# One decoder layer with retention in chunks of 128, transposes by halves, and gates and biases of the down product in front of the first expert

## The chip, the cores and the metric

The kernel runs on one core of a Trainium2 chip. The metric is device time in microseconds (us), the median over the runs of one execution each: 1484.77 us for the kernel before, in three runs between 1484.51 and 1488.26.

## The reference, cut to what matters

One layer over 512 tokens of width 1024, in float32. Eight heads of 64 do stick-breaking attention and eight do retention; their outputs share one output projection. Then a mixture of 32 experts, four per token, and a gate on a second input of 256 per token.

```python
xn = rmsnorm(x); proj = xn @ w_in                    # 1024 -> 7 * 512
sb_q, sb_k, sb_v, r_q, r_k, r_v, r_g = split(proj)   # 512 columns each, 8 heads of 64
y_a = stick_breaking(rmsnorm(sb_q), rmsnorm(sb_k), sb_v)
y_b = retention(rope(rmsnorm(r_q)), rope(rmsnorm(r_k)) / 8, r_v)
y_b = group_norm(y_b) * silu(r_g)                    # mean and variance over a head's 64
x = x + concat(y_a, y_b) @ w_out
hn = rmsnorm(x)
x = x + moe(hn)                                      # top 4 of 32, clamped SwiGLU, 1024 wide
x = x + (p @ w_ple_proj) * sigmoid(rmsnorm(x) @ w_ple_gate)

def retention(q, k, v):                              # per head, chunks of c = 128, g = 1 - 2**(-5-h)
    inner = (q k^T * dmat) v                         # dmat[i, j] = g**(i-j) for i >= j, else 0
    kv    = (k * g**(c-1-j))^T v                     # 64 x 64 per chunk
    state = g**c * state + kv                        # scan over the chunks
    cross = (q state_before) * g**(i+1)
    return inner + cross

def moe(xt):
    gates = softmax(top_k(xt @ w_router + b_router, 4))
    for each expert e, for its tokens xb:
        glu, lin = split(xb @ w_up_gate[e] + b_up_gate[e])   # 1024 -> 2 * 1024
        h = min(glu, 7) * sigmoid(1.702 * min(glu, 7)) * (clip(lin, -7, 7) + 1)
        y[tokens] += gate * (h @ w_down[e] + b_down[e])      # 1024 -> 1024
```

## The kernel before

**In front of the experts.** The tokens are four tiles of 128 (NT = 4), the heads are paired (NP = 4 pairs of 64 + 64 partitions). A projection is done in three products of rounded halves (`mm3`, L163 to L165: high by high, low by high, high by low), and the halves of the weights are split on ScalarE and VectorE (L158, L159). In this part the scheduler of the tile framework sets the order on each engine from dependences and priorities, so the order of the program text is not the order of the engines. The pieces around the change are, in the order in which TensorE comes to them:

- `ret_qk` (L326) projects the retention queries and keys, takes each head's norm (`headnorm_rstd`, tile rrk), rotates them on VectorE (tiles nrk, mrk) and transposes them to rqT and rkT (`to_T`). For the queries the norm's factor is multiplied on here (L343); for the keys it is kept as the column rkr.
- `val` projects the values (tiles pjvR from the split weights wsvR0 to wsvR7); L580 to L582 subtract each head's mean over its 64 values, which is the mean that the group norm would take off.
- The retention loop (L593 to L632) runs over the pairs. For every chunk b of 128 keys it makes a score product rz of these keys with all queries from b on, so 512, 384, 256 and 128 columns (L607); VectorE multiplies it by the key's factor and by dec (L613), which ScalarE makes as an exponential of dif, the distance with a large value where the key is later; and a product ry with the values adds to the pair's output over the same columns (L618). The pair's two heads stand on different halves of the array's rows or columns. Then come the square (rsq), its mean per head as a product with a constant (var, L625), two table functions, gain, bias and the gate gD, and the split into yB.
- `wo_half` (L635) is the output projection. Its first half (on yA, from the attention, tiles pjo, 96 matmuls) needs nothing of the retention, and the scheduler fills it in between; the second half needs yB. The halves of its weights are woh and wol.

**The experts.** From L857 on the four compute engines run in the order in which the program is written (`manual_schedule`). Expert e has its tokens gathered to C = 96 rows (`dispatch`: a product rk spreads the ranks, VectorE makes the indices, GpSimd gathers xg from hn_d). Its 12 MiB of weights come in six pieces of 2 MiB into a ring of nine slots; pieces 0 to 3 are the up product's and 4 and 5 the down product's. `load_behind(e, c)` issues, on SyncE's queue, the load of the piece that takes over the slot of piece c, so a load begins once the products that read this slot are done.

- `turn` (L914) transposes xg in two halves of four 128-column blocks (px), each copied to xT by ScalarE; `turn_in` (L1081) does it for the next expert while the current one is at work.
- `up` (L1092) is glu and lin of the first 64 tokens, and `up32` (u) that of the other 32, where an expert has over 64 tokens. `act_in` and `act_out` make h on VectorE and ScalarE.
- `h_T` (L1149) transposes a half of h (two blocks, ph) and VectorE copies it to hT; `down` (L1157) multiplies by w_down (yb), `down32` the other 32 (yc).
- The transposes take their PSUM bank from `dbank` (L887), which hands out banks 2 and 3 in turn.
- `gates_T` (L841) transposes the gates of a tile of 128 tokens (pg, into gt), and `down_bias` (L849) adds the experts' down biases to the sum acc as a product of gt with the 32 biases bd (pb). Tiles 0 and 1 are done ahead of the loop; tiles 2 and 3 at its beginning: the transposes behind the row transposes of expert 0, the products inside its up product (L1301, L1304). `rows_of_y` makes, on VectorE, the row numbers by which each token later collects its experts' outputs.

The order in an expert is: up, act, up32, loads behind pieces 0 to 3, both halves of the next expert's row transposes, first half of h, two down products of four pairs, second half of h, the next two, act32, dispatch of the expert after next, the last four, rows out, down32, loads behind pieces 4 and 5.

## Time and profile before

| | before |
|---|---|
| median of three runs | 1484.77 us |
| profiled execution, device time | 1485.39 us |
| its span | 1483.5 us |
| PE busy | 91% |
| DVE (VectorE) busy | 30% |
| ACT (ScalarE) busy | 20% |
| POOL (GpSimd) busy | 12% |
| DMA, mean over the span | 320 GB/s |
| granted TensorE clock, mean | 0.985 |

All trace numbers are of this one profiled execution, 1485.39 us by the clock of the runs and 1483.5 us from its first to its last instruction. PE is a matmul on TensorE. A float32 matmul leaves two records in the trace (one per pass), one in the rounded format leaves one. The granted clock is a share of full speed: 1.00 is 2.4 GHz and 0.50 is 1.2 GHz. In a timeline a row is a start, a length, the engine, the line, the operation with the tiles out<-in, their shapes, how many records the row gathers, and in brackets how long the engine had stood idle before it and what ended that. Ends of matmuls are modelled, and the next one begins before the end of the last; so a run of matmuls is measured from start to start.

### The profile page before, as it was taken

Reading aid. Unit: us, or ns where it says so; the run is one execution under the profiler, and the core shown is the slowest. Engines: PE = TensorE matmul, PEld = TensorE weight load, DVE = VectorE, ACT = ScalarE, POOL = GpSimd, SP = SyncE. Lnnn points to the kernel's source line nnn. Section 1 sums busy time; section 2 is a strip of 40 time slices with the busy share of each in tenths; the row PEclk is TensorE's granted clock in tenths of the full one; section 3 lists DMA queues with packets and bytes.
Section 4 is the critical chain, followed back from the end, with each engine's and each line's share of the span. In section 5 each row is a group of like instructions: output and inputs, shape, how many; then the busy total and the mean of one; then the engine's idle time right before and its main releaser. Section 6 shows DMA issues by size and latency. Waiting matters only on the chain. (4 is left out here: it accounts for less than half of the span.)

```text
span 1483.5 us, 21634 instructions
## 1 busy us (share of the span) xinstructions
PE 1353.6 (91%) x8629; PEld 652.0 (44%) x8629; DVE 451.4 (30%) x1033; ACT 293.3 (20%) x564; POOL 182.4 (12%) x268
## 2 busy tenths in 40 slices
PE   8999999997999999999988899878999889799788
PEld 6776775463333334334333333323333333233256
DVE  4657497545111111111211111111111121032353
ACT  5645674341010000000000001000000000111133
POOL 3132000011110111010101011000111100212230
PEclk9999999998999999999999999999999999999999
DMA  7202504167999999999999999999999999989931
GB/s 286 85 29 79 143 25 170 38 250 278 362 375 410 408 390 403 413 411 414 412 392 411 410 408 412 411 397 417 408 410 394 374 413 408 398 346 403 420 131 57
DMA packets 65528, 474.81 MB, mean 320 GB/s; under 512 B 9485, under 2 KB 10033, under 8 KB 32401
## 3 DMA queue, kind: packets, MB, share of 16 engines
q1 hardware_dynamic: 54192, 441.69, 74.7%
q0 software_dynamic: 11200, 31.22, 6.0%
q8 instruction: 97, 1.59, 0.4%
q14 instruction: 39, 0.31, 0.1%
HBM read 454.40 MB, written 18.48 MB: 319 GB/s over the span
## 5 line engine op out<-in xcount | busy, mean ns | idle before, releaser
L1161 PE MATMUL yb<-ring,hT 128*64 128x512 f32 x1024 | 245.6, 612 | 35.3 <-DVE hT L1154 27.4
L1103 PE MATMUL glu<-ring,xT 128*64 128x512 f32 x1024 | 247.6, 599 | 16.3 <-DMA ring<-in_w_up_gate_dram 16.3
L1103 PE MATMUL lin<-ring,xT 128*64 128x512 f32 x1024 | 245.5, 594 | 0.0
L1139 DVE TENSOR_SCALAR gl<-glu 128x512 f32<-128x512 f32 x32 | 22.1, 692 | 530.7 <-PE glu L1103 530.7
L1103 PEld LDWEIGHTS glu<-ring,xT 128*64 128x64 f32 x1024 | 81.9, 138 | 145.5 <-issue 115.8
L1103 PEld LDWEIGHTS lin<-ring,xT 128*64 128x64 f32 x1024 | 83.0, 137 | 139.5 <-issue 139.5
L1161 PEld LDWEIGHTS yb<-ring,hT 128*64 128x64 f32 x1024 | 65.7, 137 | 152.8 <-issue 100.8
L903 POOL DMA_INDIRECT xg<-hn_d,idx x32 | 30.5, 954 | 781.3 <-DVE idx L902 469.0
L1117 PE MATMUL u<-ring,xT 128*32 128x256 f32 x2048 | 113.3, 379 | 0.0
L1140 ACT ACTIVATE sg<-gl 128x512 f32<-128x512 f32 x32 | 20.1, 629 | 408.8 <-DVE gl L1139 408.8
L1117 PEld LDWEIGHTS u<-ring,xT 128*32 128x32 f32 x2048 | 61.6, 110 | 47.4
L1174 PE MATMUL yc<-ring,hv 128*32 128x256 f32 x1024 | 58.6, 381 | 8.3 <-DVE hv L1170 8.3
L1185 ACT COPY y<-yb 128x512 f32<-128x512 f32 x31 | 18.1, 585 | 231.9 <-PE yb L1161 222.1
L920 ACT COPY xT<-px 128x384 f32<-128x384 f32 x64 | 27.7, 482 | 155.5 <-PE px L919 155.4
L1174 PEld LDWEIGHTS yc<-ring,hv 128*32 128x32 f32 x1024 | 31.6, 110 | 31.3 <-DVE hv L1170 12.1
L919 PE MATMUL px<-ident,xg 96*128 96x96 f32 x256 | 28.9, 258 | 15.4 <-PEq L1314 8.1
L1187 POOL DMA_DIRECT2D y_d<-y x62 | 33.7, 548 | 68.7 <-ACTq L1334 39.1
L919 PEld LDWEIGHTS px<-ident,xg 96*128 96x128 f32 x256 | 23.2, 145 | 34.9 <-issue 24.2
L1181 POOL DMA_DIRECT2D y_d<-yv x64 | 31.6, 501 | 54.5 <-ACT yv L1179 48.4
L1403 PE MATMUL o<-gh,z 128*128 128x512 f32 x128 | 37.3, 400 | 0.2 <-ACT z L1360 0.2
L899 DVE SCALAR_TENSOR_TENSOR scr<-rk,slot,iot 96x512 bf16<-96x512 f32 x32 | 23.9, 746 | 40.9 <-PE rk L893 40.9
L1141 DVE TENSOR_TENSOR gl<-gl,sg 128x512 f32<-128x512 f32 x32 | 22.2, 692 | 24.4 <-ACT sg L1140 23.7
(960 smaller groups left out, 1694.5 us busy)
## 6 DMA issues: line engine op xcount, KB each, us to landing
ring<-in_w_up_gate_dram SPq DMA_DIRECT2D x127, 2048.0 KB, 23.6
ring<-in_w_down_dram SPq DMA_DIRECT2D x128, 1024.0 KB, 23.0
ring<-in_w_in_dram SPq DMA_DIRECT2D x12, 1024.0 KB, 5.3
y_d<-y POOLq DMA_DIRECT2D x62, 128.0 KB, 9.7
ring<-in_w_out_dram SPq DMA_DIRECT2D x4, 1024.0 KB, 6.7
ring<-in_w_ple_gate_dram SPq DMA_DIRECT2D x2, 2048.0 KB, 22.0
y_d<-none SPq DMA_DIRECT2D x2, 1984.0 KB, 12.0
ring<-in_x_dram SPq DMA_DIRECT2D x4, 512.0 KB, 5.4
```

The lines of the kernel that those rows point to most:

```text
L899: nc.vector.scalar_tensor_tensor(scr[0:n], rk[0:n], slots[0:n], iot[0:n], op0=ALU.is_equal, op1=ALU.mult, accum_out=idf[0:n])
L903: nc.gpsimd.indirect_dma_start(out=xg[0:n], out_offset=None, in_=hn_d, in_offset=bass.IndirectOffsetOnAxis(ap=idx[0:n, :1], axis=0))
L919: nc.tensor.transpose(pv[:, k, :], xg[0:n, (4 * h + k) * P:(4 * h + k + 1) * P], ident[0:n, 0:n])
L920: nc.scalar.copy(xT[:, 4 * h:4 * h + 4, 0:n], pv)
L1103: nc.tensor.matmul(o[two(j)], xTs[e][:, 2 * m + c, 0:64], w[:, c, f:f + 512], start=False, stop=m == 3 and c == 1)
L1117: nc.tensor.matmul(u32[four(q), g * 256:(g + 1) * 256], xTs[e][:, 2 * m + c, 64:C], w[:, c, f:f + 256], start=False, stop=m == 3 and c == ...
L1141: nc.vector.tensor_tensor(gl, gl, sg, op=ALU.mult)
L1161: nc.tensor.matmul(y64[two(j)], hT[:, fc, :], w[:, fc % 4, j * 512:(j + 1) * 512], start=fc == 0, stop=fc == KD - 1)
L1174: nc.tensor.matmul(y32[four(q), 0:256], hT[:, fc % 2, fc // 2, :], w[:, fc % 4, q * 256:(q + 1) * 256], start=fc == 0, stop=fc == KD - 1, ...
L1181: nc.gpsimd.dma_start(y_d[e * C + 64:(e + 1) * C, q * 256:(q + 1) * 256], y[four(q)])
L1187: nc.gpsimd.dma_start(y_d[e * C:e * C + 64, j * 512:(j + 1) * 512], y[two(j)])
L1403: nc.tensor.matmul(banks[t, h], (zh, zl, zh)[i][:, k, ts], (g_h, g_h, g_l)[i][k // 4][:, k % 4, hs], start=first, stop=last)
```

## The change

**Retention.** The keys get their factor on VectorE before the transposes, and both queries and keys an exponential of the place in the chunk besides (`decay`: g to the plus place for queries, g to the minus place for keys), multiplied into the eight small columns of the norm (L332). So neither the column rkr nor the exponentials dec are needed. A score product is one chunk of 128 by itself (L629), four per head in one bank, and VectorE multiplies a head's four by one mask of zeros and ones (`causal`). The rest goes over states: for chunks 0 to 2, eight products of 64 by 64 (kv, L609) from the unturned keys and the values, with the sum and the factor `tile_decay` on VectorE (st); a cross product per head and chunk from 1 on (L638) and an inner product per head and chunk (L644) write the pair's output, 128 columns each. Square, var and what follows stay.

**Gates and biases.** `gates_T` and `down_bias` of tiles 2 and 3 stand ahead of the row transposes of expert 0, and the two calls inside its up product are gone.

**Transposes in halves.** `turn_in` takes a half h; the order is now first half of the next rows, first half of h, second half of the rows, second half of h, and then all eight pairs of the down product in one piece. `dbank` turns over three banks, 2 to 4.

```diff
     def ret_qk(w, name, key, tag, ahead=0):
         ns = evacuate(proj(w, name, ahead), name)
         dst = early.tile([P, NP, S], F32, name=name + "T", tag=tag)
-        rst = early.tile([P, NT, NH], F32, name=name + "r")
         for t in range(NT):
             n = ns[t]
-            r, _ = headnorm_rstd(n, f"{name}{t}", rst[:, t, :])
+            r, _ = headnorm_rstd(n, f"{name}{t}")
+            nc.vector.tensor_tensor(r, r, decay[key], op=ALU.mult)
...
             nc.vector.tensor_tensor(n, n, m, op=ALU.add)
-            if key == "q":
-                nc.vector.tensor_tensor(nv, nv, r[:, :, None].to_broadcast([P, NH, HD]), op=ALU.mult)
+            nc.vector.tensor_tensor(nv, nv, r[:, :, None].to_broadcast([P, NH, HD]), op=ALU.mult)
             to_T(n, dst, t, None, f"{name}{t}")
-        return dst, rst
+        return dst, ns
...
-    dif = early.tile([P, S], F32, name="dif")
-    nc.gpsimd.iota(dif, pattern=[[1, S]], base=0, channel_multiplier=-1, allow_small_or_imprecise_dtypes=True)
-    msk = e2.tile([P, S], F32, name="msk", tag="tmp")
-    nc.vector.tensor_scalar(msk, dif, 0.0, 1.0e6, op0=ALU.is_lt, op1=ALU.mult)
-    nc.vector.tensor_tensor(dif, dif, msk, op=ALU.add)
+    lng = [math.log(1.0 - 2.0 ** (-5.0 - h)) for h in range(NH)]
+    place_col = early.tile([P, 1], F32, name="place_col")
+    nc.gpsimd.iota(place_col, pattern=[[0, 1]], base=0, channel_multiplier=1, allow_small_or_imprecise_dtypes=True)
+    decay = {}
+    for key, sign in (("q", 1.0), ("k", -1.0)):
+        decay[key] = early.tile([P, NH], F32, name="decay" + key)
+        for h in range(NH):
+            nc.gpsimd.memset(decay[key][:, h:h + 1], sign * lng[h])
+        nc.scalar.activation(decay[key], decay[key], AF.Exp, scale=place_col)
+    tile_decay = early.tile([P, NP], F32, name="tile_decay")
+    for h in range(NH):
+        nc.gpsimd.memset(tile_decay[h % 2 * HD:h % 2 * HD + HD, h // 2:h // 2 + 1], math.exp(P * lng[h]))
+    causal = early.tile([P, P], F32, name="causal")
+    nc.vector.tensor_scalar(causal, jp, 0.0, None, op0=ALU.is_ge)
...
-    rkT, rkr = ret_qk(w_rk, "rk", "k", "kT", 200)
+    rkT, rkn = ret_qk(w_rk, "rk", "k", "kT", 200)
...
+    hss = [slice(j * HD, (j + 1) * HD) for j in range(2)]
+    kvb = [bank(6 + i, f"kv{i}") for i in range(2)]
+    states = []
+    for b in range(NT - 1):
+        kv = kvb[b // 2][:, b % 2 * 256:b % 2 * 256 + 256]
+        for h in range(NH):
+            nc.tensor.matmul(kv[hss[h % 2], h // 2 * HD:h // 2 * HD + HD], rkn[b][:, h * HD:(h + 1) * HD],
+                             vR[:, b, h * HD:(h + 1) * HD], start=True, stop=True)
+        st = e2.tile([P, 256], F32, name=f"st{b}", tag=("wt1", "wt1", "wt2")[b])
+        sv = st.rearrange("p (c d) -> p c d", d=HD)
+        fall = tile_decay[:, :, None].to_broadcast([P, NP, HD])
+        if b == 0:
+            nc.vector.tensor_tensor(sv, kv.rearrange("p (c d) -> p c d", d=HD), fall, op=ALU.mult)
+        else:
+            nc.vector.tensor_tensor(st, states[-1], kv, op=ALU.add)
+            nc.vector.tensor_tensor(sv, sv, fall, op=ALU.mult)
+        states.append(st)
     for hp in range(NP):
-        hss = [slice(j * HD, (j + 1) * HD) for j in range(2)]
-        decs = []
+        py = bank(4 + hp % 2, f"ry{hp}")
+        zs, scs = [], []
         for j in range(2):
-            h = 2 * hp + j
-            dec = e2.tile([P, S], F32, name=f"dec{h}", tag="tmp")
-            nc.scalar.activation(dec, dif, AF.Exp, scale=math.log(1.0 - 2.0 ** (-5.0 - h)))
-            decs.append(dec)
-        py = bank(4 + hp % 2, f"ry{hp}")
+            zs.append(zbank(f"rz{hp}{j}", (0, 1, 2, 3)))
         for b in range(NT):
-            N = S - b * P
-            zs, scs = [], []
+            ts = slice(b * P, (b + 1) * P)
             for j in range(2):
-                z = zbank(f"rz{hp}{j}{b}", (0, 1, 2, 3))
-                nc.tensor.matmul(z[:, :N], rkT[hss[j], hp, b * P:(b + 1) * P], rqT[hss[j], hp, b * P:S],
-                                 start=True, stop=True)
-                zs.append(z)
+                nc.tensor.matmul(zs[j][:, ts], rkT[hss[j], hp, ts], rqT[hss[j], hp, ts], start=True, stop=True)
+        for j in range(2):
+            sc = e2.tile([P, S], F32, name=f"rs{2 * hp + j}", tag="wt0")
+            nc.vector.tensor_tensor(sc.rearrange("p (b t) -> p b t", t=P), zs[j].rearrange("p (b t) -> p b t", t=P),
+                                    causal[:, None, :].to_broadcast([P, NT, P]), op=ALU.mult)
+            scs.append(sc)
+        for b in range(1, NT):
+            ts = slice(b * P, (b + 1) * P)
+            for j in range(2):
+                nc.tensor.matmul(py[hss[j], ts], states[b - 1][hss[j], hp * HD:(hp + 1) * HD], rqT[hss[j], hp, ts],
+                                 start=b == 1, stop=False)
+        for b in range(NT):
+            ts = slice(b * P, (b + 1) * P)
             for j in range(2):
                 h = 2 * hp + j
-                sc = e2.tile([P, N], F32, name=f"rs{h}{b}", tag=f"wt{b}")
-                nc.vector.scalar_tensor_tensor(sc, zs[j][:, :N], rkr[:, b, h:h + 1], decs[j][:, :N],
-                                               op0=ALU.mult, op1=ALU.mult)
-                scs.append(sc)
-            for j in range(2):
-                h = 2 * hp + j
-                nc.tensor.matmul(py[hss[j], b * P:S], vR[:, b, h * HD:(h + 1) * HD], scs[j],
-                                 start=b == 0, stop=b == NT - 1)
+                nc.tensor.matmul(py[hss[j], ts], vR[:, b, h * HD:(h + 1) * HD], scs[j][:, ts], start=False,
+                                 stop=b == NT - 1)
...
     def down_bias(t):
         for h in range(2):
-            pb = bank(h + (6 if t > 1 else 4), f"pb{t}{h}")
+            pb = bank(h + (6 if t == 2 else 4), f"pb{t}{h}")
...
     def dbank(name):
         dn[0] += 1
-        return bank(2 + dn[0] % 2, name)
+        return bank(2 + dn[0] % 3, name)
...
-    def turn(xg, n, xT, name):
-        for h in range(2):
+    def turn(xg, n, xT, name, halves=range(2)):
+        for h in halves:
             pt = dbank(f"px{name}{h}")
...
-    def turn_in(e):
-        xTs[e] = ringC.tile([P, KD, C], F32, name=f"xT{e}", tag="xT")
-        turn(xgs[e], C, xTs[e], f"{e}")
+    def turn_in(e, h):
+        if e < E:
+            if h == 0:
+                xTs[e] = ringC.tile([P, KD, C], F32, name=f"xT{e}", tag="xT")
+            turn(xgs[e], C, xTs[e], f"{e}", (h,))
...
+    for t in (2, 3):
+        gates_T(t)
+    for t in (2, 3):
+        down_bias(t)
     turn(xgs[0], C, xTs.setdefault(0, ringC.tile([P, KD, C], F32, name="xT0", tag="xT")), "0")
-    gates_T(2)
-    gates_T(3)
     for t in range(NT):
         rows_of_y(t)
...
         up(e, 0)
-        if e == 0:
-            down_bias(2)
         up(e, 1)
-        if e == 0:
-            down_bias(3)
...
         for c in range(4):
             load_behind(e, c)
-        if e + 1 < E:
-            turn_in(e + 1)
+        turn_in(e + 1, 0)
         h_T(h, hT, 0, f"{e}a")
-        down(e, hT, (0, 1))
+        turn_in(e + 1, 1)
         h_T(h, hT, 1, f"{e}b")
-        down(e, hT, (2, 3))
+        down(e, hT, (0, 1, 2, 3))
```

VectorE around the last splits of the value weights (wsvR5l to wsvR7l), before; nrk and mrk are tiles of the rotated keys, vm the means of the values:

```order
L159 SCALAR_TENSOR_TENSOR wsvR5l<-ring_62,pmix,wsvR5h 128x512
L341 TENSOR_TENSOR nrk_1996<-nrk_1996,mrk_2039 128x512
L338 TENSOR_TENSOR mrk_2055<-nrk_1998,stk 128x8x32
L340 TENSOR_TENSOR nrk_1998<-nrk_1998,ctk 128x512
L341 TENSOR_TENSOR nrk_1998<-nrk_1998,mrk_2055 128x512
L159 SCALAR_TENSOR_TENSOR wsvR6l<-ring_62,pmix,wsvR6h 128x512
L159 SCALAR_TENSOR_TENSOR wsvR7l<-ring_62,pmix,wsvR7h 128x512
L580 TENSOR_REDUCE vm_2216<-vR 128x8
L580 TENSOR_REDUCE vm_2220<-vR 128x8
```

The same place after (rrk is the norm's factor of a key tile, wol a split of the second output weight):

```order
L159 SCALAR_TENSOR_TENSOR wsvR5l<-ring_62,pmix,wsvR5h 128x512
L341 TENSOR_TENSOR nrk_2031<-nrk_2031,mrk_2081 128x512
L332 TENSOR_TENSOR rrk_2095<-rrk_2095,decayk 128x8
L338 TENSOR_TENSOR mrk_2100<-nrk_2033,stk 128x8x32
L342 TENSOR_TENSOR nrk_2031<-nrk_2031,rrk_2076 128x512
L340 TENSOR_TENSOR nrk_2033<-nrk_2033,ctk 128x512
L159 SCALAR_TENSOR_TENSOR wsvR6l<-ring_62,pmix,wsvR6h 128x512
L341 TENSOR_TENSOR nrk_2033<-nrk_2033,mrk_2100 128x512
L581 TENSOR_TENSOR wol_2252<-ring_63,woh_2251 128x1024
L342 TENSOR_TENSOR nrk_2033<-nrk_2033,rrk_2095 128x512
L159 SCALAR_TENSOR_TENSOR wsvR7l<-ring_62,pmix,wsvR7h 128x512
L589 TENSOR_REDUCE vm_2262<-vR 128x8
```

A factor of eight columns and a multiply over 512 columns of each key tile, and a split of wol, now stand between the splits.

TensorE behind the last value product, before:

```order
L165 MATMUL pjvR_2071<-wsvR7h,xl 128x512
L607 MATMUL rz_2259<-rqT,rkT 128x512
L607 MATMUL rz_2261<-rqT,rkT 128x512
L607 MATMUL rz_2269<-rqT,rkT 128x384
L607 MATMUL rz_2271<-rqT,rkT 128x384
L163 MATMUL pjo_2482<-woh_2205,yA 128x512
L164 MATMUL pjo_2482<-wol_2206,yA 128x512
L618 MATMUL ry_2258<-rs_2263,vR 64x512
L607 MATMUL rz_2279<-rqT,rkT 128x256
L165 MATMUL pjo_2482<-woh_2205,yA 128x512
L618 MATMUL ry_2258<-rs_2265,vR 64x512
```

The same place after (kv are the products of keys and values, st the states):

```order
L165 MATMUL pjvR_2117<-wsvR7h,xl 128x512
L629 MATMUL rz_2335<-rqT,rkT 128x128
L629 MATMUL rz_2336<-rqT,rkT 128x128
L629 MATMUL rz_2335<-rqT,rkT 128x128
L629 MATMUL rz_2336<-rqT,rkT 128x128
L609 MATMUL kv_2300<-vR,nrk_2027 64x64 x8
L629 MATMUL rz_2335<-rqT,rkT 128x128
...
L629 MATMUL rz_2376<-rqT,rkT 128x128 x4
L609 MATMUL kv_2300<-vR,nrk_2029 64x64 x8
L609 MATMUL kv_2301<-vR,nrk_2031 64x64 x8
L638 MATMUL ry_2334<-rqT,st_2310 64x128 x2
L629 MATMUL rz_2377<-rqT,rkT 128x128 x4
```

Products of 128 to 512 columns with pjo between them have become runs of 128 columns, with states and cross products in front of the first pjo.

TensorE in expert 0, its start and the turn from up to down product, before (px are transposed rows, pg gates, pb biases, ph transposes of h):

```order
L919 MATMUL px_3095<-ident,xg_3041 128x96 x4
L919 MATMUL px_3101<-ident,xg_3041 128x96 x4
L845 MATMUL pg_3108<-ident,gates 96x128
L845 MATMUL pg_3113<-ident,gates 96x128
...
L852 MATMUL pb_3209<-bd_2632,gt_3107 128x512
L852 MATMUL pb_3212<-bd_2632,gt_3107 128x512
...
L919 MATMUL px_3329<-ident,xg_3054 128x96 x4
L919 MATMUL px_3335<-ident,xg_3054 128x96 x4
L1153 MATMUL ph0a<-ident,h_3194 128x128 x2
L1161 MATMUL yb_3191<-ring_2602,hT_3195 64x512 x4
L1153 MATMUL ph0b<-ident,h_3194 128x128 x2
L1161 MATMUL yb_3191<-ring_2602,hT_3195 64x512 x4
```

and after:

```order
L871 MATMUL pg_3111<-ident,gates 96x128
L871 MATMUL pg_3116<-ident,gates 96x128
L878 MATMUL pb_3120<-bd_2648,gt_3110 128x512
L878 MATMUL pb_3123<-bd_2648,gt_3110 128x512
...
L945 MATMUL px_3133<-ident,xg_3057 128x96 x4
L945 MATMUL px_3139<-ident,xg_3057 128x96 x4
...
L945 MATMUL px_3345<-ident,xg_3070 128x96 x4
L1181 MATMUL ph0a<-ident,h_3222 128x128 x2
L945 MATMUL px_3355<-ident,xg_3070 128x96 x4
L1181 MATMUL ph0b<-ident,h_3222 128x128 x2
L1189 MATMUL yb_3219<-ring_2618,hT_3223 64x512 x8
```

Gates and biases have moved ahead of the rows; each pair of transposes of h has a half of the next rows ahead of it, and the down product is no longer cut by one.

## Rows read from the trace of the kernel before

**Rows 1.** The page's forty slices, DMA line: busy share in tenths.

```profile
DMA  7202504167999999999999999999999999989931
```

**Rows 2.** Windows, PE: stretch, length, busy (x instructions), granted clock, DMA share, GB/s.

```profile
236.08:299.18 63.10, 61.36 (x233) 1.00 0.39 137
...
340.90:349.40 8.50, 2.60 (x18) 0.50 0.65 208
```

**Rows 3.** Groups, PE, 236.08 to 299.18: busy, mean ns, idle before, releaser.

```profile
L618 PE MATMUL ry<-rs,vR 128*64 128x512 f32 (+3 forms) x64 | 18.1, 458 | 1.4 <-DVE rs L613 1.4
L607 PE MATMUL rz<-rqT,rkT 64*128 64x256 f32 (+3 forms) x64 | 17.0, 473 | 0.0
...
L625 PE MATMUL var<-rsq,gmean 128*128 128x512 f32 x8 | 4.4, 634 | 0.3 <-ACT rsq L623 0.3
```

**Rows 4.** Timeline, PE: start, length, engine, line, operation, tiles.

```profile
84.33 1.05 PE L442 MATMUL prs<-ident,rs 128*128 128x128 f32 x8
...
283.07 0.43 PE L618 MATMUL ry<-rs,vR 128*64 128x128 f32 x2
283.43 0.50 PE L165 MATMUL pjo<-woh,yA 128*128 128x512 f32 x1
...
291.02 0.40 PE L164 MATMUL pjo<-wol,yA 128*128 128x512 f32 x1
...
298.95 0.40 PE L165 MATMUL pjo<-woh,yA 128*128 128x512 f32 x1
```

**Rows 5.** Windows and timeline, DVE, projection of retention keys and values.

```profile
208.30:228.80 20.50, 19.81 (x32) 1.00 0.01 1
...
198.75 0.69 DVE L343 TENSOR_TENSOR nrq<-nrq,rqr 128x512 f32<-128x512 f32 x1
...
231.35 0.75 DVE L159 SCALAR_TENSOR_TENSOR wsvR7l<-ring,pmix,wsvR7h 128x512 fp32r<-128x512 f32 x1 [2.54 <-ACT wsvR7h L158]
```

**Rows 6.** Windows, PE, of the holes in the stream.

```profile
365.00:372.00 7.00, 7.00 (x100) 1.00 0.26 66
404.00:409.00 5.00, 5.00 (x88) 1.00 0.38 88
441.00:444.00 3.00, 1.84 (x16) 1.00 0.65 158
...
1127.00:1131.00 4.00, 4.00 (x74) 1.00 0.73 279
1164.00:1168.00 4.00, 1.65 (x11) 0.85 0.66 233
1297.00:1305.00 8.00, 6.83 (x38) 1.00 0.41 123
```

**Rows 7.** Timeline, PE, start of expert 0.

```profile
347.10 1.51 PE L919 MATMUL px<-ident,xg 96*128 96x96 f32 x8 [5.90 <-DMA xg<-hn_d,idx]
...
354.17 0.73 PE L852 MATMUL pb<-bd,gt 96*128 96x512 f32 x2
...
359.32 1.09 PE L852 MATMUL pb<-bd,gt 96*128 96x512 f32 x2 [0.83 <-DVE acc L854]
```

**Rows 8.** Timeline, PE, turn from up to down in expert 1.

```profile
412.95 0.44 PE L1153 MATMUL ph1a<-ident,h 128*128 128x128 f32 x2 [0.29 <-ACT xT L920]
413.91 1.94 PE L1161 MATMUL yb<-ring,hT 128*64 128x512 f32 x8 [0.52 <-DVE hT L1154]
...
416.73 1.94 PE L1161 MATMUL yb<-ring,hT 128*64 128x512 f32 x8 [0.52 <-DVE hT L1154]
```

**Rows 9.** Timelines, PE and DVE, expert 28.

```profile
1302.12 0.85 PE L919 MATMUL px<-ident,xg 96*128 96x96 f32 x8 [0.31 <-PEq L1314]
...
1302.65 0.42 DVE L1147 SCALAR_TENSOR_TENSOR h<-h,gl 128x256 f32<-128x256 f32 x1
```

**Rows 10.** Waits, PE, 370 to 1425: total, count, longest; timeline, expert 31.

```profile
PE glu L1103 <- DMA ring<-in_w_up_gate_dram: 16.3, 10, 2.6
...
1386.82 1.94 PE L1103 MATMUL glu<-ring,xT 128*64 128x512 f32 x8 [2.57 <-DMA ring<-in_w_up_gate_dram]
```

## The prediction, made before the changed kernel was run

> **What bounds the kernel now.** I began with the DMA line of the forty slices [rows 1]: the 16 DMA engines are nearly idle in slices 6 to 8 and full from the tenth slice to the last but two. That long stretch is the expert loop, which streams 12 MiB of weights per expert. A kernel that is full on DMA for two thirds of its time can shorten in three ways only: the stream begins earlier, it has fewer holes, or the part behind it shrinks. So I read three places. First the stretch in front of the loop, where TensorE (PE) is the bound: from 236.08 to 299.18 PE is busy for 61.36 of 63.10 us while DMA is at 0.39 [rows 2]. Then the start of the loop, where PE stands idle for the first gather (2.60 us busy of 8.50, at half the clock [rows 2]). Then the holes in the stream, cut out by windows [rows 6]; every one ends when a ring slot is released, and slots 0 to 3 of an expert are released by its up product, so by PE. The loop's end is tied to the stream: expert 31 waits 2.57 us for its weights [rows 10], and over the whole loop PE waits 16.3 us for weights, in ten waits, all of them after 760 us (the view gives the same row when it begins there) [rows 10]. So before 760 us PE sets when slots come free, and what it gains there closes holes; whatever shifts the stream shifts the end.
>
> **The retention stage.** In the 63.1 us, 96 matmuls of the first half of the output projection (pjo, the filler) step by 7.93/34 = 0.233 us [rows 4], together 22.4; waits are 1.4 + 0.3 us [rows 3]; so retention itself holds PE for 39.0 us, and the three groups rz, ry, var read 18.1 + 17.0 + 4.4 = 39.5 [rows 3]. The change replaces 64 matmuls of 128 to 512 columns by 32 score tiles, 24 state products, 24 cross and 32 inner products, 112 small ones, and keeps var. A float32 matmul leaves two records, one for each pass, so x8 in a row is four of them. Prices: four 128-column float32 matmuls in a run take 1.05 us to the last one's end, 0.25 each with the pipeline's end taken off [rows 4]; a lone one takes 0.36 until the next kind starts (283.07 to 283.43) [rows 4], so a change of kind costs about 0.11. Two matmuls on different halves of the array run together when they stand side by side (the 64 records of the score products by 473 ns would be 30.3 us and take 17.0 [rows 3]); in the order of the changed kernel 8 pairs and 16 lone score tiles, 12 pairs of cross, 16 of inner and 12 of state products do. So 24 + 12 + 16 + 12 = 64 turns by 0.25 = 16.0, var 4 by 1.1 = 4.4, and 30 changes of kind (57 before) by 0.11 = 3.3: 23.7 us, 15.3 less. The Trainium skill, page TensorEngine Tiling (Array Packing), section Key Properties, states that a change of tiling mode drains TensorE; the 0.11 agrees with that, and without it the sum would be 3.3 us lower.
>
> The bounds: with no cost for a change of kind 39.0 - 20.4 = 18.6 us are saved; with all 112 alone at 0.36, 40.3 + 4.4 = 44.7, 5.7 are lost. I take 15.3, since the order has most of them in runs. What hides the rest: the chain behind the last inner product (copy, square, var, two table functions, two vector operations, split) needs some 8 us, an estimate, and has 79 pjo by 0.233 = 18.4 us in front of it, so it stays covered. The eight exponentials and the 17 us of score scaling that go on ScalarE and VectorE lay beside PE and give nothing. One us I charge for new waits: state products wait for the centred values, cross products for the states on VectorE, which stands behind two splits of the second output weight.
>
> **The price in front of it.** The key rows now get their scale on VectorE, four more 128x512 multiplies at 0.69 [rows 5], 2.8 us, and four tiny ones. VectorE is busy for 19.81 of 20.50 us there and then has 2.54 us of air before the split of the last value weights [rows 5]. PE takes these splits as they come, and key transposes now wait for one operation more. Walking the two queues by these durations I find waits of 0.3 to 0.8 us at four places: 2 us, between 0 and 3.3. ScalarE's two small exponentials and the 24 extra fills of GpSimd at the start lie in idle time and cost nothing. The stage: 15.3 - 1 - 2 = 12 us earlier, between -9 and 19.
>
> **Gates and down biases ahead of expert 0.** Before, PE waits 5.90 us for the gather, then transposes rows, then gates, and the biases stand inside the up product: 0.73 us at 354.17, and 0.83 of waiting plus 1.09 at 359.32 [rows 7], of whose 2.65 I take 2.5, since the last pass of each runs into the next matmul. Now all this stands in the wait. The gates of the last two tiles are ready before the gather lands; at half the clock the work ends about 1 us after it, which is what the gates cost behind the transposes before. So up begins at the same time and ends 2.5 us earlier, the first slots with it; bounds 1.5 and 2.5. Nothing on VectorE is later: the bias additions move ahead of the rows of y.
>
> **Transposes in halves.** In an expert with over 64 tokens the down product waited for 0.29 (second bank of xT), 0.52 and 0.52 us (hT copies) [rows 8]; now each copy has a half of the transposes or another product over it, and three banks turn: 1.33 us less. In a light expert h comes from VectorE after the up product: its first half is ready at about 1303.05, when four transposes from 1302.12 would be done at 1302.55 [rows 9]; half a us of wait is new, so 0.86 remains. PE is not the bound everywhere, so this counts through holes alone. They lose (1 - share) times length [rows 6]: 5.2 at 365, 3.1 at 404, 1.0 at 441, 1.1 at 1127, 1.4 at 1164, 4.7 at 1297, together 16.5. The first shrinks by the 2.5 of expert 0; the next two by 1.3 and 1.0, since PE is then 1.3 us further ahead per expert; those at 1127 and 1164 stand behind three and four heavy experts in a row, 3.9 and 5.2 us of gain against 2.5, and go; of the last I take half, 2.3, as PE may run into the stream in the light experts ahead of it. 2.5 + 2.3 + 2.5 + 2.3 = 9.6, taken as 10; bounds 2.5 (expert 0 alone) and 14.
>
> **The sum.** 12 + 10 = 22 us. The profiled execution took 1485.39 us (span 1483.5), 0.6 over the median of 1484.77; 1485.4 - 22 = 1463.4, and 1463 against the median.
>
> **Rivals.** A measurement of this kernel tells about 0.3% (4.5 us) from no change.
> - Stream-bound: the holes stay, because DMA is at its limit and PE only waits in other places. For it speaks the full share between the holes; against it that each hole ends with a release by PE. Then 12 + 2.5: 1485.4 - 14.5 = 1471.
> - Better packing: changes of kind cost little in runs and the hole at 1297 closes. 19 + 14 = 33: 1452.
> - Lone matmuls: the small products don't overlap and pay 0.36 each; the stage is 5.7 + 3 = 9 slower, the loop gives 10 back: 1484, no change.
> - Slower: the cross products wait for states, these for VectorE, and PE idles between so many short products that its granted clock falls, as it does in 340.9 to 349.4 (0.50, with 2.60 us busy of 8.50 [rows 2]). The stage's 48 us at 1.2 GHz cost up to 48 more: 1463 + 48 = 1511; it decides from 22 us at the lower level. Against it: by my walk no wait in the stage is over 1 us. The Trainium skill, page TensorE: Matmul & The Clock Gate, Part 1, has the lower rate as the one an idle engine falls back to.
> - That the change does not do what it says is settled by the order: small products, halves and gates stand where the text puts them.
>
> **How the numbers follow.** Forecast 0.55 (1463, own range 1455 to 1471), stream-bound 0.18, better packing 0.16, lone matmuls 0.08, slower clock 0.03. Faster takes the first three and a corner of the fourth, 0.90; same 0.06; slower 0.04. The range reaches from the better packing to just past the stream-bound case: 1452 to 1474.
>
> **What will show it.** In the changed profile the stretch from the last value product to the last pjo of the first half should be 49 to 51 us instead of 63; the value products should be pushed back by about 2 us with waits for VectorE; glu of expert 0 should begin about 12 us earlier than 349.4 and its up product hold no bias; waits of the down product for hT should all but vanish; the DMA share at the six holes should be near 1 save the first two. I am wrong if the short products take over 0.3 us a turn, if PE's clock falls in the stage, or if the holes move instead of closing.

## The result, and the profile after

The changed kernel takes 1460.85 us (median of four runs, 1459.98 to 1462.05); the kernel before took 1486.01 beside it. The ratio is 0.983, 95% interval 0.9813 to 0.9847. The forecast was 1463. The profiled execution has a span of 1458.8 us against 1483.5, so 24.7 us are to be found.

I cut both spans at five instructions whose starts stand in the TensorE timelines: the first score product, the first product of the second half of the output projection, the first bias product of expert 0, the first product of expert 31 with its weights, and the end. The same cuts serve for every kernel below.

| us | before | after | change |
|---|---|---|---|
| up to the first score product | 236.1 | 237.1 | +1.1 |
| retention stage | 63.1 | 45.0 | -18.1 |
| from there to the loop's start | 50.2 | 50.8 | +0.6 |
| loop, to the first weights of expert 31 | 1037.4 | 1028.3 | -9.1 |
| tail | 96.7 | 97.5 | +0.8 |

The page's clock and DMA lines of after, in forty slices; the DMA line answers to [rows 1]:

```profile
PEclk9999999998999999999999999999999999899889
DMA  8201604549999999999999999999999999999921
```

The full stretch of DMA begins a slice earlier and has no dip left up to the last slice but two. The clock has new dips in three of the last six slices.

Windows on TensorE after, columns as in [rows 2]: the retention stage, and the wait in front of expert 0.

```profile
237.14:282.20 45.06, 44.39 (x330) 1.00 0.60 211
...
325.00:333.00 8.00, 4.92 (x18) 0.50 0.76 245
```

The stage holds TensorE for 44.39 of 45.06 us. Its groups (busy, mean ns, idle before them), of which the first three and the last take the place of rz and ry in [rows 3]:

```profile
L629 PE MATMUL rz<-rqT,rkT 64*128 64x128 f32 x64 | 6.9, 291 | 0.0
L644 PE MATMUL ry<-rs,vR 128*64 128x128 f32 x64 | 5.2, 280 | 0.0
L638 PE MATMUL ry<-rqT,st 64*64 64x128 f32 x48 | 4.6, 285 | 0.0
L651 PE MATMUL var<-rsq,gmean 128*128 128x512 f32 x8 | 4.3, 618 | 0.5 <-ACT rsq L649 0.5
...
L609 PE MATMUL kv<-vR,nrk 128*64 128x64 f32 x48 | 2.0, 227 | 0.2 <-DVE vR L591 0.2
```

Together 23.0 us, where [rows 3] had 39.5. The start of expert 0 after, in the timeline, which answers to [rows 7]:

```profile
328.07 1.40 PE L871 MATMUL pg<-ident,gates 128*96 128x128 f32 x4 [3.41 <-DVE gates L847]
329.48 2.30 PE L878 MATMUL pb<-bd,gt 96*128 96x512 f32 x4
331.57 1.48 PE L945 MATMUL px<-ident,xg 96*128 96x96 f32 x8
...
333.84 3.26 PE L1131 MATMUL glu<-ring,xT 128*64 128x512 f32 x8
```

The wait is now for the gates, 3.41 us; the rows follow gates and biases. The turn from up to down product in expert 1 after, against [rows 8]:

```profile
391.49 0.55 PE L945 MATMUL px<-ident,xg 96*128 96x96 f32 x4
391.87 0.39 PE L1181 MATMUL ph1a<-ident,h 128*128 128x128 f32 x2
392.09 0.49 PE L945 MATMUL px<-ident,xg 96*128 96x96 f32 x4
392.66 0.44 PE L1181 MATMUL ph1b<-ident,h 128*128 128x128 f32 x2
393.03 3.65 PE L1189 MATMUL yb<-ring,hT 128*64 128x512 f32 x16
```

The two waits of 0.52 us are gone, and of the one of 0.29 some 0.07 are left, ahead of row 392.66; the sixteen records of the down product follow each other. Over a whole expert TensorE needs 35.2 instead of 36.9 us with over 64 tokens, and 25.1 instead of 26.1 with fewer (starts of the bias products of neighbouring experts).

The windows of the holes that are left, against [rows 6]:

```profile
349.00:354.00 5.00, 5.00 (x94) 1.00 0.37 95
385.00:389.00 4.00, 4.00 (x80) 1.00 0.55 156
1262.00:1264.00 2.00, 1.97 (x13) 1.00 0.74 268
1270.00:1276.00 6.00, 5.11 (x28) 1.00 0.65 244
```

(1 - share) times length gives 3.2, 1.8, 0.5 and 2.1 us, 7.6 together, where [rows 6] gave 16.5. What TensorE waits for weights over the span, total, times and longest, against [rows 10]:

```profile
PE glu L1131 <- DMA ring<-in_w_up_gate_dram: 46.9, 24, 8.1
```

So the loop's TensorE time fell by some 42 us (16 times 1.7 and 15 times 1.0), and 30.6 us of that are new waits for weights.

### The profile page after: what moved, and what is told of

It is laid out like the page before. It is cut to its first block, busy times and chain, and to the rows that moved or that the text cites. A ratio compares the mean times of both kernels' runs of the same rounds, so it can differ in the third digit from the quotient of the medians.

```text
span 1458.8 us, 21861 instructions
## 1 busy us (share of the span) xinstructions
PE 1339.0 (92%) x8725; PEld 656.6 (45%) x8725; DVE 446.8 (31%) x1025; ACT 291.7 (20%) x558; POOL 185.7 (13%) x292
## 5 line engine op out<-in xcount | busy, mean ns | idle before, releaser
L1131 PE MATMUL glu<-ring,xT 128*64 128x512 f32 x1024 | 258.0, 624 | 46.9 <-DMA ring<-in_w_up_gate_dram 46.9
L1189 PE MATMUL yb<-ring,hT 128*64 128x512 f32 x1024 | 235.4, 602 | 0.8 <-DVE hT L1182 0.8
L929 POOL DMA_INDIRECT xg<-hn_d,idx x32 | 30.6, 957 | 765.6 <-DVE idx L928 424.1
L946 ACT COPY xT<-px 128x384 f32<-128x384 f32 x64 | 30.7, 480 | 163.4 <-PE px L945 161.9
L945 PE MATMUL px<-ident,xg 96*128 96x96 f32 x256 | 33.8, 255 | 6.5 <-PEq L1341 4.6
L945 PEld LDWEIGHTS px<-ident,xg 96*128 96x128 f32 x256 | 25.7, 143 | 26.4 <-PEq L1341 16.2
```

Of the source, the lines that this page charges most:

```text
L929: nc.gpsimd.indirect_dma_start(out=xg[0:n], out_offset=None, in_=hn_d, in_offset=bass.IndirectOffsetOnAxis(ap=idx[0:n, :1], axis=0))
L945: nc.tensor.transpose(pv[:, k, :], xg[0:n, (4 * h + k) * P:(4 * h + k + 1) * P], ident[0:n, 0:n])
L946: nc.scalar.copy(xT[:, 4 * h:4 * h + 4, 0:n], pv)
L1131: nc.tensor.matmul(o[two(j)], xTs[e][:, 2 * m + c, 0:64], w[:, c, f:f + 512], start=False, stop=m == 3 and c == 1)
L1189: nc.tensor.matmul(y64[two(j)], hT[:, fc, :], w[:, fc % 4, j * 512:(j + 1) * 512], start=fc == 0, stop=fc == KD - 1)
```

## The experiments

The first six kernels are the other combinations of the three parts, so that with before and after all eight are there. Four kernels then test single prices and waits, and two the place of the instructions.

| kernel | median us | ratio to before, interval | stage | loop | tail |
|---|---|---|---|---|---|
| before | 1484.6 to 1486.4 | | 63.1 | 1037.4 | 96.7 |
| retention alone | 1466.18 | 0.9875 (0.9847 to 0.9902) | 45.0 | 1032.8 | 98.4 |
| halves alone | 1479.75 | 0.9957 (0.9941 to 0.9972) | 63.1 | 1033.1 | 94.8 |
| gates alone | 1485.96 | 1.0004 (0.9990 to 1.0017) | 63.1 | 1038.4 | 96.2 |
| retention, halves | 1461.82 | 0.9841 (0.9819 to 0.9863) | 45.0 | 1030.0 | 98.5 |
| retention, gates | 1466.41 | 0.9867 (0.9845 to 0.9888) | 45.0 | 1032.5 | 98.4 |
| halves, gates | 1477.55 | 0.9943 (0.9921 to 0.9966) | 63.1 | 1030.7 | 94.7 |
| all three (after) | 1460.85 | 0.9830 (0.9813 to 0.9847) | 45.0 | 1028.3 | 97.5 |

**Retention alone.** The changed kernel with the old calls put back for the other two parts:

```diff
-    for t in (2, 3):
-        gates_T(t)
-    for t in (2, 3):
-        down_bias(t)
...
+    gates_T(2)
+    gates_T(3)
...
         turn_in(e + 1, 0)
+        turn_in(e + 1, 1)
         h_T(h, hT, 0, f"{e}a")
-        turn_in(e + 1, 1)
+        down(e, hT, (0, 1))
         h_T(h, hT, 1, f"{e}b")
-        down(e, hT, (0, 1, 2, 3))
+        down(e, hT, (2, 3))
```

> The kernel before with the tiled retention alone; transposes, gates and biases stand as before. Theory A (a shift in front counts in full, and the PE time saved in the loop counts only as far as it closes holes of the stream): the loop starts some 17 us earlier as in the changed kernel, its six holes stay, together about 19 us, so 1486.0 - 16.5 = 1469.5. Theory B (only the front counts; what PE saves in the loop is waited away for weights): as fast as the whole change, 1461. Theory C (packing gains little, and the loop brings most): over 1476.

1466.18, 19.0 us less than the kernel before beside it (1485.21), and 3 us less than A. The front is as A has it (loop at 333.3 against 349.4). But the loop, in which nothing was changed, is 4.6 us shorter. Windows of its last three holes:

```profile
1110.00:1114.00 4.00, 4.00 (x68) 1.00 0.79 299
1147.00:1149.00 2.00, 1.41 (x12) 1.00 0.82 262
1278.00:1283.00 5.00, 4.45 (x27) 1.00 0.69 225
```

0.8, 0.4 and 1.6 us: the earlier holes are about those of [rows 6], but these three lose 2.8 where [rows 6] had 1.1 + 1.4 + 4.7 = 7.2. B falls: 1466 is not 1461. C falls too.

**Halves alone.** The kernel before with the order and the three banks of the changed one:

```diff
-        return bank(2 + dn[0] % 2, name)
+        return bank(2 + dn[0] % 3, name)
...
-            turn_in(e + 1)
+        turn_in(e + 1, 0)
         h_T(h, hT, 0, f"{e}a")
-        down(e, hT, (0, 1))
+        turn_in(e + 1, 1)
         h_T(h, hT, 1, f"{e}b")
-        down(e, hT, (2, 3))
+        down(e, hT, (0, 1, 2, 3))
```

> The kernel before with the transposes in halves over three banks alone. A: an expert with over 64 tokens takes 35.2 us on PE instead of 36.9, one with fewer 25.1 instead of 26.1; the loop starts where it did, at 349.4; the holes at 404, 441, 1127 and 1164 close and half of that at 1297, about 7 us: 1479. B: 1486, no change, and the waits of the up product for weights grow by as much as PE saves, some 35 us. C: 1476 or less.

1479.75, as A says; the loop is 4.3 us shorter and the tail 1.9. The waits for weights do grow, from 14.3 to 44.4 us up to the first weights of expert 31, as B said as well: both hold, most of the gain is waited away and what closes holes stays. A is wrong on the last hole, though:

```profile
1288.00:1300.00 12.00, 11.06 (x53) 1.00 0.46 169
```

It loses 6.5 us, where [rows 6] had 4.7.

**Gates alone.** The kernel before with

```diff
+    for t in (2, 3):
+        gates_T(t)
+    for t in (2, 3):
+        down_bias(t)
     turn(xgs[0], C, xTs.setdefault(0, ...), "0")
-    gates_T(2)
-    gates_T(3)
...
-        if e == 0:
-            down_bias(2)
...
-        if e == 0:
-            down_bias(3)
```

> The kernel before with gates and down biases ahead of the first expert's row transposes alone. A: up of expert 0 is 2.2 us shorter and the first hole shrinks by that: 1483.8, too little to tell from no change in the time, so the trace of the first hole (365 to 372 before) decides: 3 us lost in it instead of 5.2. B: 1486, with the first hole smaller and another larger.

1485.96, no difference. The windows of its first and its last hole:

```profile
365.00:370.00 5.00, 5.00 (x96) 1.00 0.44 118
...
1294.00:1306.00 12.00, 10.84 (x50) 1.00 0.23 65
```

The first hole loses 2.8 us (5.2 before), as A has it, but the last one loses 9.2 (4.7 before). So it went as B says: the gain of 2.4 us at the beginning is taken back at the end. Experts 24 and 26 are 1.5 and 2.9 us longer there than in the kernel before; on these see below.

**Retention and halves.** The changed kernel with the last diff undone.

> The changed kernel with the gates and biases back in their old places. A: 1460.9 + 2.2 = 1463, the first hole of the stream larger by 2.2 us than in the changed kernel. B: 1461, no difference.

1461.82 against 1460.85; the intervals overlap widely. The traces differ by 1.7 us in the loop, but by the time A and B can't be told apart.

**Retention and gates.** The changed kernel with the diff of the halves undone.

> The changed kernel with the transposes in the old order over two banks. A: the holes that the halves close come back, some 7 us: 1468. B: 1461, no difference, since PE only waits less for weights.

1466.41: B falls, and A is 1.6 us high, as it was 3 us high with the retention alone, whose late holes this kernel shares.

**Halves and gates.** The kernel before with both of these diffs.

> The kernel before with gates and halves, without the tiled retention. A: the loop starts at 349.4 as before and its holes shrink from 19 to about 9 us: 1476.5. B: 1486.

1477.55, as A says, with the loop at 1030.7.

**Pairs apart.** The changed kernel with the loops over the two heads of a pair turned outside in, in all four kinds of products, as here for the scores:

```diff
-        for b in range(NT):
-            ts = slice(b * P, (b + 1) * P)
-            for j in range(2):
+        for j in range(2):
+            for b in range(NT):
+                ts = slice(b * P, (b + 1) * P)
```

> The changed kernel with each pair's first head written out ahead of its second one, so that two products on different halves of the array no longer stand side by side (scores, cross, inner and state products). If two such products run together and a pair costs one turn of 0.25 us, as the forecast has it, some 45 turns more are paid: 10 to 12 us, 1471 to 1473. If a product on half of the array costs its own time wherever it stands: 1461, and the retention stage stays at 45 us.

1461.5, ratio 0.9832 (0.9815 to 0.985), no difference in the time; the stage has 48.4 us instead of 45.0. Eight inner products (16 records) and the next row, first of this kernel, then of the changed one:

```profile
249.39 1.58 PE L644 MATMUL ry<-rs,vR 128*64 128x128 f32 x16
250.90 0.87 PE L638 MATMUL ry<-rqT,st 64*64 64x128 f32 x8
```

```profile
248.04 1.09 PE L644 MATMUL ry<-rs,vR 128*64 128x128 f32 x16
249.06 0.43 PE L638 MATMUL ry<-rqT,st 64*64 64x128 f32 x4
```

From start to start 1.51 us apart and 1.02 side by side: 0.19 us for a product alone and 0.255 for a pair. So pairs do run together, the pair's price of 0.25 was right, and the price of a product alone was not: 0.25 came from products over the whole array [rows 4], 0.19 is that of one on half of it. Some 48 fewer pairs cost 3.4 us of the stage: TensorE is busy for 48.39 us in it instead of 44.39, and 0.7 us of waits are gone. The loop starts 3.8 us later; the tail takes 1.2 of that back, and the profiled span is 2.5 us longer. The medians are only 0.65 us apart; the four runs of this kernel spread over 2.8 us, so the time alone can't show the 2.5.

**Work in the wait for the gates.** Twelve products of 512 columns from 32 rows, read by nothing:

```diff
+    warm(bank(0, "warm0"), 12)
     for t in (2, 3):
         gates_T(t)
```

> The changed kernel with 12 products of 512 columns, whose result nothing reads, on PE in the 3.4 us in which it waits for the gates of the last two tiles. If the half clock behind that idle time is what makes gates, biases and the first up products slow (0.50 from 325 to 333, 0.74 to 340), the clock stays near 1.00, the first up product is released some 2.3 us earlier and the first hole of the stream shrinks by that: 1458.6. If the hole is set by something else: 1461.

1460.07, ratio 0.9829 (0.981 to 0.9848), no difference. The timeline there:

```profile
324.86 5.48 PE L935 MATMUL warm<-rankT,ident_r 32*128 32x512 f32 x12
...
333.55 1.49 PE L949 MATMUL px<-ident,xg 96*128 96x96 f32 x8
...
335.82 2.19 PE L1135 MATMUL glu<-ring,xT 128*64 128x512 f32 x8
```

The twelve take 5.48 us, 0.46 each: the clock had fallen before they began, and it did not rise under them (0.50 from 325 to 335). They end 2.0 us too late for gates, biases and rows. In return the first up products run at full clock sooner. The test did not keep the clock up, so what that would be worth at expert 0 stays open.

**The place of the instructions.** In the kernel before and in the three others with the old retention, the row transposes in one to three light experts (64 tokens or fewer) are held up, mostly by TensorE's sequencer. A row of expert 24 before, and the sum of the sequencer's waits there over the loop (total, times, longest), before and with the retention alone:

```profile
1166.62 1.35 PE L919 MATMUL px<-ident,xg 96*128 96x96 f32 x8 [2.35 <-PEq L1314]
```

```profile
PE px L919 <- PEq L1314: 8.1, 14, 2.4
```

```profile
PE px L945 <- PEq L1343: 4.6, 15, 0.3
```

These waits lie at the branch over the 32-token part. Experts 18, 24 and 26 take 29.4, 30.5 and 28.9 us before, and 26.1 each with the retention alone. About half of that is the clock: behind each wait the next eight records of the down product take 3.60, 3.68 and 3.42 us, and not 1.94. At expert 24 (granted clock 0.50 from 1167 to 1173):

```profile
1169.16 3.68 PE L1161 MATMUL yb<-ring,hT 128*64 128x512 f32 x8 [0.52 <-DVE hT L1154]
```

The wait of expert 24 stands inside the hole at 1164, and all three ahead of the largest late one, at 1297. Two kernels test whether it is the place of TensorE's instructions that makes them. The first adds 12 products of 64 columns to the retention alone, in front of the first rows; the second 96 to the kernel before:

```diff
+    shift(bank(0, "shift"))
     turn(xgs[0], C, xTs.setdefault(0, ringC.tile([P, KD, C], F32, name="xT0", tag="xT")), "0")
```

> The tiled retention alone (1466.2) with 12 products of 64 columns, read by nothing, ahead of the first row transposes, in PE's wait for the gather. They move every later PE instruction of the program by 12 products. In the kernels with the old retention PE's sequencer holds the row transposes of experts 18, 24 and 26 up for 1.5 to 2.8 us each behind the branch over the 32-token part; with the new retention no such wait is over 0.3 us, and the loop is 4.6 us shorter although nothing in it was changed. If the place of the instructions decides this, the waits of 1.5 us or more come back here and the loop (1032.8 us from its start to the first weights of expert 31) grows to about 1037: 1470. If it is something that the retention does, nothing changes: 1466.

1467.16, ratio 0.9883 (0.9854 to 0.9913), and the loop 1032.2: the time does not change, and experts 18, 24 and 26 have no wait over 0.8 us. But the rows of experts 12 and 14 now wait 1.74 and 1.44 us, where they don't with the retention alone. The view puts these waits down to VectorE and not to the sequencer, so a sum by the sequencer's name misses them:

```profile
PE px L949 <- DVE h L1178: 1.7, 1, 1.7
```

> The kernel before with 96 such products, by which the new retention leaves more PE records than the old one (8725 against 8629), in the wait for the gather. If the place of the instructions decides: the waits of PE's sequencer at experts 18, 24 and 26 fall to 0.3 us and the loop goes from 1037.4 to about 1033, 1481.5 in all, less what the 96 products push the row transposes back (0 to 2 us). If not: 1485 to 1488, with the waits of 1.5 to 2.8 us as they were.

1500.83, ratio 1.0111 (1.0079 to 1.0142). The 96 products took far longer than I had thought, 0.216 us each:

```profile
340.34 20.69 PE L909 MATMUL shift<-rankT,ident_r 32*128 32x64 f32 x96
```

They push the loop's start back by 13.9 us; the profiled span is 12.7 us longer and the median 16.2. The loop is 1.7 us shorter (1035.7) and not the 4.4 that I had expected, since the up product of expert 0, which frees the first slots, comes later and DMA moves nothing from 361 to 372. But the waits at experts 18, 24 and 26 are gone, and with them most of the late holes, 1.2 + 0.4 + 1.6 = 3.1 us instead of 7.2:

```profile
PE px L923 <- PEq L1319: 4.3, 14, 0.3
```

```profile
1143.00:1147.00 4.00, 4.00 (x72) 1.00 0.71 270
1180.00:1182.00 2.00, 1.40 (x11) 1.00 0.81 254
1311.00:1316.00 5.00, 3.83 (x24) 1.00 0.68 219
```

The kernel with work in the wait for the gates, which is the changed one with 12 products more, waits 2.91 us at expert 12 and 2.76 at expert 18. The changed kernel itself has one such wait, of 1.58 us at expert 12, for which the trace shows no releaser ("issue"; the other of the two lies under 0.4):

```profile
PE px L945 <- issue: 1.9, 2, 1.6
```

Taken whatever the view names, these are the waits over 1 us at row transposes inside the loop, in the one execution of each kernel that was profiled. The last column is the DMA time lost from the start of expert 24 to that of expert 30: 1 less the DMA share, summed over the microseconds with a share under 0.9.

| kernels | waits: expert (us) | DMA time lost, us |
|---|---|---|
| before | 18 (1.94), 24 (2.35), 26 (1.48) | 7.0 |
| gates alone | 18 (1.97), 24 (2.19), 26 (2.02) | 11.3 |
| halves alone; halves, gates | 26 (2.76; 2.67) | 7.2; 6.9 |
| retention alone | none | 3.3 |
| retention, gates | 2 (2.17) | 3.3 |
| retention, halves; after; pairs apart; the two with work at the end (below) | 12 (1.51 to 1.87) | 2.4 to 3.1 |
| work in the wait for the gates | 12 (2.91), 18 (2.76) | 3.0 |
| retention alone, 12 products ahead | 12 (1.74), 14 (1.44) | 3.1 |
| before, 96 products ahead | 2 (2.08) | 2.7 |

So in these traces products put ahead of the loop move the waits from one expert to another. That the waits at 18, 24 and 26 can go without the new retention is shown by the 96 products. The late holes go with waits at experts 24 and 26: 6.9 to 11.3 us are lost in the four kernels that have one there, 2.4 to 3.3 in the ten that have none. Whether the waits move with the place of the instructions or with the time by which the products shift the rest is not told apart: the 12 products ahead of the retention alone bring two with the loop's start unmoved (333.2 against 333.3), which speaks against the time, but the other two kernels shift it by 13.9 and 2.0 us. With one trace of each it is not shown either that a kernel has them at the same expert in every execution; that five kernels have theirs at expert 12 speaks for it.

**Work in the waits at the end.** Products that nothing reads at three places of expert 31 where TensorE idles:

```diff
+        if e == E - 1:
+            warm(bank(5, "warm1"), 34)
         glu, lin, u32 = bank(0, f"glu{e}"), ...
...
+        if e == E - 1:
+            warm(dbank("warm2"), 14)
         with tc.If(n_e > 64):
...
         if e == E - 1:
+            warm(bank(5, "warm3"), 12)
             break
```

> The changed kernel with products that nothing reads where PE idles at the end: 34 of 512 columns ahead of expert 31, in its 8.1 us wait for weights, 14 in the wait for its activation, 12 behind its down product. If the clock falls there because PE idles (0.70 from 1361 to 1366, 0.76 from 1387 to 1396, 0.85 to 1404), it stays near 1.00 and the tail from expert 31's first weights to the end shrinks from 97.5 to about 94: 1457.5. If not, or if the products come in the way of real ones: 1461 or more.

1464.15, ratio 0.9856 (0.9828 to 0.9884), 3.3 us slower than the changed kernel. The first window, and the first up product behind it:

```profile
1353.00:1366.00 13.00, 13.00 (x38) 0.57 1.03 432
```

```profile
1364.64 3.62 PE L1135 MATMUL glu<-ring,xT 128*64 128x512 f32 x8
```

TensorE is busy without a gap and its granted clock falls all the same, to 0.57 in the mean; at half the clock the products outlast the wait by 3 us. The products used 32 of the 128 rows. So I changed that, and with it the operands (the identity on both sides) and the numbers, to 28, 10 and 10:

```diff
-            nc.tensor.matmul(pb, ident_r[0:E, 0:1].to_broadcast([E, P]), rankT, start=True, stop=True)
+            nc.tensor.matmul(pb, ident_r, ident_r[:, None, :].to_broadcast([P, 4, P]), start=True, stop=True)
```

> The changed kernel with products that nothing reads where PE idles at the end, as in the kernel before this one (1464, where the clock fell to 0.57 although PE was busy all the time with products over 32 of the 128 rows), but over all 128 rows: 28 ahead of expert 31, 10 in the wait for its activation, 10 behind its down product. If the clock goes with how much of the array is at work, it stays at 1.00 from 1352 to 1404 and the tail behind expert 31's first weights shrinks from 97.5 to about 94: 1457.5. If it falls all the same: 1462 or more, as the products then last beyond the wait.

1461.57, ratio 0.9829 (0.9811 to 0.9846). Windows, and the rows of the products, the down product and the join behind it (pc, by which expert 31's output is added to its tokens):

```profile
1353.00:1360.00 7.00, 6.26 (x30) 1.00 1.03 431
1360.00:1366.00 6.00, 3.91 (x12) 0.72 1.00 425
...
1387.00:1396.00 9.00, 8.83 (x40) 1.00 0.78 313
```

```profile
1352.11 6.59 PE L935 MATMUL warm<-ident_r 128*128 128x512 f32 x28 [0.57 <-PEq L1370]
...
1387.17 7.09 PE L1193 MATMUL yb<-ring,hT 128*64 128x512 f32 x32 [1.24 <-DVE hT L1186]
...
1399.24 0.98 PE L1232 MATMUL pc<-yl,oh 64*128 64x512 f32 x4 [2.45 <-DVEq L1466]
```

With all rows at work the clock stays at 1.00 until the products end, and falls at the end of the 2.84 us that are then left of the wait for weights (0.72). That the rows decide, and not the values in the operands, is likely but not shown. The down product runs at 1.00. The same window, and the first up product, the down product and the join, in the changed kernel:

```profile
1387.00:1396.00 9.00, 8.69 (x32) 0.76 0.76 304
```

```profile
1361.27 3.28 PE L1131 MATMUL glu<-ring,xT 128*64 128x512 f32 x8 [8.13 <-DMA ring<-in_w_up_gate_dram]
...
1387.32 9.06 PE L1189 MATMUL yb<-ring,hT 128*64 128x512 f32 x32 [0.79 <-DVE hT L1182]
1399.19 0.83 PE L1228 MATMUL pc<-yl,oh 64*128 64x512 f32 x4 [2.81 <-DVEq L1457]
```

The down product is 2.0 us shorter (7.09 against 9.06 us), and the join begins at 1399.24 against 1399.19: nothing gained. VectorE, which adds the collected rows of the other experts, ends that work there only at 1398.4, and the split of expert 31's output that the join reads (yl, 0.68 us) stands behind it in VectorE's order (its timeline in the kernel with all rows):

```profile
1393.57 4.86 DVE L1268 SCALAR_TENSOR_TENSOR acc<-gy,gk,acc 128x1024 f32<-128x1024 f32 x4
```

My 1457.5 was wrong at this step. I had taken TensorE for the last in the tail, and at the join it is VectorE.

## Why the prediction was right, point by point

**The stage.** Forecast 63.1 - 15.3 + 1 = 48.8 us, measured 45.0, below the 49 to 51 that I had named as a sign. Taking off 96 products of the filler at 0.233 (22.4) and 0.7 us of waits leaves 21.9 for the retention, where 23.7 was forecast; the rest of the 3.8 us are waits, of which I had kept the old 1.7 and added one, and found 0.7. So the mechanism was right, and two terms were a little high. The state products were the cheapest against their price: 2.0 us by their group, where 12 turns of 0.25 had been put down for them. The 0.11 us for a change of kind made 3.3 of the 23.7; without it the sum was 20.4, and 21.9 lies between. The Trainium skill, page TensorEngine Tiling (Array Packing), section Key Properties, has a change of tiling mode drain TensorE, and tiles on different parts of the array work in parallel; the pairs (0.255 against twice 0.19) agree with the second, and no run here takes the first apart from the rest.

**In front of it.** Forecast +2 us, measured +1.1; over all traces the first score product starts at 235.2 to 236.1 us with the old retention and at 237.0 to 237.9 with the new one, 1.7 us apart in the mean. The next stretch is 0.6 longer, and so the loop starts 16.4 us earlier where 12 was forecast.

**Expert 0.** Rows came about a us behind the gather, as forecast: 331.57, with the gather's landing put at 330.55 (as far behind the last product ahead of the wait as before, 6.18 us). Up then ran at half the clock longer: its first eight records need 3.26 us. From the loop's start to the end of the 64-token up product it is 16.1 us instead of 18.0, so 1.9 of the 2.5 are left. Alone the part brings nothing that shows.

**The halves.** Forecast 1.33 and 0.86 us an expert, measured 1.7 and 1.0; the down product in one piece gains besides the waits.

**The holes.** Forecast -10 for the loop, measured -9.1, and hole for hole: 3.2 at the first (forecast 5.2 - 2.5 = 2.7), 1.8 at the second (1.8), none at 441, 1127 and 1164, half of the last. The rule behind it held in all eight combinations: TensorE time in the loop is worth what it closes of holes. The loop takes 1028.3 to 1038.4 us in them; less its lost DMA time, counted as above over the whole loop, it takes 1016.7 to 1020.9. But the account by parts was wrong. I put all of the 10 down to gates and halves; alone they shorten the loop by -1.0 and 4.3 us, and the retention, which I gave none of it, by 4.6, of which 4.4 lie in the three late holes. These holes go with the waits at experts 24 and 26, in all fourteen kernels. The trace of the kernel before shows these waits (8.1 us in all, up to 2.4 at a time), one of them inside the very hole of which I wrote that a row of heavy experts was behind it. So the step that was wrong is the cause of the late holes. I had put half of the last one down to the halves; alone they leave it at 6.5 us (4.7 before), and the retention brings it to 1.6, along with the waits at experts 24 and 26, of which I had not thought. That the loop's sum came out all the same is luck.

**The tail.** I forecast no change; it is 0.8 us longer. Expert 31 waits 8.1 us for its first weights instead of 2.57 [rows 10], and its first up product and its down product then run at a reduced clock.

**The rivals.** Stream-bound (1471) falls by the halves, which bring 6.4 us alone (0.9957), and by the holes, of which 7.6 us are left of 16.5; but most of the 42 us that are saved on TensorE is indeed waited away. Lone matmuls (1484) falls by its price: apart, the products cost 3.4 us and not 21. The slower clock (1511) falls by the stage's granted clock of 1.00. Better packing (1452) was right on the stage (-18.1 of its 19) and wrong on the loop.

## What to carry to other kernels

Where a stream of weights is the bound for most of the time, look for its holes and for what each waits; time in front of the stream counts in full, compute time beside it only as far as it closes a hole. A forecast whose sum is right may still be wrong by parts: the eight combinations of three edits showed that 4.6 us of the loop come through a part that was not meant to touch it. Price a matmul on half of the array from one on half of the array.

## What was unexpected of the hardware

- The granted clock fell to 0.50 while TensorE was busy without a gap, with products of 512 columns from 32 rows (mean 0.57 over 13.00 us, all busy); with products of the same columns from all 128 rows and other operands it stayed at 1.00. The Trainium skill, page TensorE: Matmul & The Clock Gate, Part 1, has the lower rate as that of an idle engine; the fall in the 2.84 us of waiting agrees, the fall under 34 products without a gap is beyond it.
- The row transposes behind the branch over the 32-token part are held up by 1.4 to 2.9 us at up to three experts of a kernel and by 0.3 at most others, and which experts these are changes with what was put hundreds of us ahead. The loss doubles where the granted clock falls behind the wait (3.68 us for eight records instead of 1.94).
- Products of 64 columns from 32 rows take 0.216 us each in a row of 96 (20.69 us) behind idle time, at a granted clock of 0.50 from the first to the last: small products are not cheap in a wait.
